# First value block of a hybrid attention block as a seven-product set, with three output gates ahead of it, and a tighter weave of side work

## The chip, the cores and the metric

The kernel runs on one core of a Trainium2 chip. The metric is the device time of one execution in microseconds (us). Matrix products run on TensorE (PE, with PEld for its loads of the stationary operand), element-wise work on VectorE (DVE) and ScalarE (ACT), small work and some DMA issues on GpSimd (POOL), and most DMA issues on SyncE (SP).

## What is computed

One layer over 256 tokens `x` of width 2048, with 256 context tokens `ctx` as a second source. All projections come from one matrix `w_in` with 19,456 columns.

```python
xn = rmsnorm(h, norm_gain[l]) * (1.0 + scale) + shift
cn = rmsnorm(hc, norm_gain[l]) * (1.0 + scale_c) + shift_c
aq, ak, av, ag, hq, hff, hfb, hi, hg, ma, mb = split_columns(xn @ w_in[l])
caq, cak, cav, cag, chq, chff, chfb, chi, chg, cma, cmb = split_columns(cn @ w_in[l])
q = apply_axial_rope(aq...) * q_scale ;  k = apply_axial_rope(ak...)
att_branch = window_attention(q, k, v, k_c, v_c, sink_logits[l]) * jax.nn.silu(ag)
g_f, k_f = hgrn_forget(hff, lb_f_all[l])          # and g_b, k_b; cg_f, ck_f; cg_b, ck_b
v_h, cv_h = to_heads(hi), to_heads(chi)
s_f = hgrn2_final_state(ck_f, cv_h, cg_f)         # start states from the context, both directions
o, _, _ = hgrn2_bidir(q_h, v_h, k_f, g_f, k_b, g_b, s_f, s_b)
hg_branch = hgrn_readout(o, hgrn_norm_gain[l], hg)
h = h + gate * merge_and_project(att_branch, hg_branch, ma, mb, ...)
return rmsnorm(h, final_norm_gain)
```

`hgrn2_bidir` is a gated linear recurrence over 16 heads in both directions, `silu(hg)` its output gate. The values `hi` are needed for the tokens and the context (512 tokens), the output gates, the merge gates `ma`, `mb` and the queries `aq` for the 256 tokens alone.

## The kernel before

**Exact products in three parts.** Every operand is split into a high part (ACT, L85: `wh`) and the rest (DVE, L86: `wl`), and a product is high x high + high x low + low x high. `proj_tok_g` (L108) computes 512 columns for some token tiles of 128: eight chunks, each one load of 512 KB by SP, one `wh`, one `wl`, and six matmuls per token tile and 128-row slice pair (L100, L101 with `wh`, L103 with `wl`). A chunk for two token tiles is a *two-token chunk*, for four a *four-token chunk*. Sums build up in PSUM banks tagged `pj`.

**Seven-product sets.** `quad_tok` (L687) computes 512 columns for all four token tiles with the seven products of Strassen's scheme in place of eight: sums of token halves, `S`, are made once by `token_sums` (DVE L586, L583, on ACT and DVE), sums of the weights by `combos` (L616), split by L635 and L636, multiplied by L732, L734 and L737 in 336 matmuls of 256 columns.

**The stages.** After the set-up of `x` and `ctx` come, in this order on PE (its order is written out by hand from L744): the first forget gates, the first value block `bv0` (512 columns, four token tiles), output gate 0 (two-token chunks; `sgg` at L535), five seven-product sets, then the other forget gates as sets. Then come eight *pairs* (two heads each, `pair`, L797, n = 0 to 7), and at the end the attention and the output projections.

**A pair.** PE transposes decay factors (`tw`), makes the context's end state (`sb`, L952), and then two *level groups* of small matmuls (L872; `al`) that build the causal matrix of the recurrence by doubling: `grow(b)` for b = 1 to 64 multiplies decay totals into `A` (DVE, two L918 for each b from 2 on), `copies` and `keep` (ACT and DVE L887) move the results. `level` 8 to 64 needs `grow` up to 32. `kt` (L978) transposes `A`, so it stands behind `grow(64)`. Then `own` (L993), DVE's L998, and `ob` (L1010 to L1012), the output.

**The weave.** `weave` (L1044) fills the places between these steps with side work for other stages: the `yield` values of `pair` are units of 12,288 PE columns, a two-token chunk is half of one. The side work (`side_work`, L1184) is a list of blocks of eight two-token chunks and one closing entry: output gates 1 to 3, merge gates (`merge_out`), attention queries (`attn_queries`: its result is rotated by DVE L1080, L1085, L1088, written to memory, and fetched back as a *task*, `tkt` at L1104) and attention gates. `SIDE` tells how many entries a pair takes; four chunks of the next pair's query projection (L154, L157) follow. Beside them run: `load_forgets`, whose `ctx_decay` issues the scans L790, L794 and L795 on DVE; `tasks_on`, at fixed entries of a pair (rotated tiles are fetched by POOL, L1139, turned by PE L1104 and written out); and the *gate steps*, one L204 on DVE for each 1.25 units of filler, each with a 256 KB fetch by POOL (`hgw`). In these pairs a query block's rotation stands where its eighth chunk falls.

Of the kernel before, what the change touches and what calls it, by code (L numbers as in the profile page):

```python
# [7 lines left out]
F32 = mybir.dt.float32  # L8
F32R = mybir.dt.float32r
U8 = mybir.dt.uint8  # L10
AF = mybir.ActivationFunctionType
# [3 lines left out]
P = 128  # L15
# [6 lines left out]
PRIO = 100000  # L22

C_Q, C_K, C_V, C_G = 0, 2048, 2560, 3072
C_HQ, C_FF, C_FB, C_HI, C_HG = 5120, 7168, 9216, 11264, 13312
# [13 lines left out]
def block_kernel(ctx: ExitStack, tc: tile.TileContext, x, c, cx, c_ctx, w_ada, b_ada, norm_gain, w_in,  # L39
                 b_merge, lb_f, lb_b, hg_gain, w_oh, sink, w_oa, w_out, fin_gain, cst, msk, out):  # L40
    nc = tc.nc
    pe, act, dve, pool = nc.tensor, nc.scalar, nc.vector, nc.gpsimd
# [6 lines left out]
    fp = ctx.enter_context(pl("fp", side="right"))  # L49
# [77 lines left out]
    def proj_tok(*a):  # L127
        return result(proj_tok_g(*a))
# [389 lines left out]
    def run(g):  # L518
        for _ in g:
            pass  # L520
# [3 lines left out]
    def send():  # L524
        while outs:
            o = outs.pop(0)
            nc.scalar.dma_start(*o[:2])
            tasks.extend(o[2:])

    def output_gate(g):  # L530
        bg = yield from proj_tok_g(w_in, C_HG + 512 * g, x_st, range(2))
        for t in range(2):
            sg = base.tile([P, 512], F32, tag="sm", name="sgg", bufs=3)
            act.activation(sg, bg[t], AF.Sigmoid)
            dve.tensor_tensor(sg, bg[t], sg, op=ALU.mult)  # L535
            outs.append((hg_dr[g][:, t * 512: (t + 1) * 512], sg))
# [24 lines left out]
    with pl("sp", reuse_waits="tile") as sp:  # L561
# [8 lines left out]
        def token_sums(g):  # L570

            def a(h, kh):
                return [X[:, 8 * kh + 4 * g: 8 * kh + 4 * g + 4, :].rearrange("p k (a h t) -> p k a h t", a=2, h=2)
                        [:, :, :, h, :].bitcast(F32) for X in (xH, xL)]

            def v(t):
                return t.rearrange("p (k a t) -> p k a t", k=4, a=2)

            def put(i, t):
                ks = slice(4 * g, 4 * g + 4)  # L580
                dst = [S[:, z, i, ks, :].rearrange("p k t -> p (k t)") for z in range(2)]
                act.activation(dst[0], t, AF.Copy)
                dve.tensor_tensor(dst[1], t, dst[0].bitcast(F32), op=ALU.subtract)  # L583

            def step(out, x_, y_, op):
                dve.tensor_tensor(out, x_, y_, op=op)  # L586

            a11, a12, a21, a22 = a(0, 0), a(0, 1), a(1, 0), a(1, 1)
            p, q = tmp(), tmp()
            step(v(p), a21[0], a22[0], ALU.add)  # L590
            step(v(q), a21[1], a22[1], ALU.add)
            step(p, p, q, ALU.add)
            put(0, p)
            step(v(q), v(p), a11[0], ALU.subtract)
            step(v(q), v(q), a11[1], ALU.subtract)
            put(1, q)
            for i, b in ((3, a12), (2, a22)):
                step(v(p), b[0], v(q), ALU.subtract)
                step(v(p), v(p), b[1], ALU.add)
                put(i, p)  # L600
# [141 lines left out]
                nc.gpsimd.dma_start(dst[t], out[t].rearrange("p a c -> p (a c)"))  # L742

        with tc.manual_schedule(engines={mybir.EngineType.PE}):  # L744
            bv0 = proj_tok(w_in, C_HI, x_st, range(4))
            for g in range(2):
                token_sums(g)
            for t in range(2):
                vo = fp.tile([P, 2, 512], F32, tag="F0", name="vo", bufs=2)
                with tc.high_priority(2 * PRIO):  # L750
                    act.activation(vo[:, 0, :], bv0[t], AF.Copy)
                    dve.tensor_copy(vo[:, 1, :], bv0[2 + t])
                nc.gpsimd.dma_start(v_dr[0][t], vo.rearrange("p a c -> p (a c)"))
            run(output_gate(0))
            send()
            for g in range(1, 4):
                quad_tok(C_HI + 512 * g, v_dr[g])
            for i, co in enumerate((C_K, C_V)):
                quad_tok(co, kv_dr[i])
            for n in range(1, 8):  # L760
                for d in range(2):
                    if (d, n) != (0, 1):
                        quad_col(d, 2 * n)
# [33 lines left out]
    def pair(g, p, F, banks_q):  # L797
# [137 lines left out]
                    pe.transpose(tw[:, (2 * i + s) * P: (2 * i + s + 1) * P], E[d][:, i, s * P: (s + 1) * P], ident)  # L935
            act.activation(wT[:, 4 * d: 4 * d + 4, :], tw.rearrange("p (a b) -> p a b", a=4), AF.Copy)
        copies(1)
        yield 2.0

        for f in done:  # L940
            f()
# [25 lines left out]
        grow(64)  # L967
        for z, b in enumerate((0, 1, 2, 4)):
            keep(a1, z * P, b)
        yield 4.0  # L970
        a3, a4 = al_bank(), al_bank()
        for al, c0, b in ((a3, 0, 8), (a3, P, 16), (a3, 2 * P, 32), (a4, 0, 64)):
            level(al, c0, b)
# [68 lines left out]
    STEP = 24 * 512  # L1042
# [82 lines left out]
    def attn_values():  # L1125
        for t in range(4):
            vr = base.tile([P, 512], F32, tag="sm", name="vr", bufs=3)
            nc.gpsimd.dma_start(vr, kv_dr[1][t % 2][:, (t // 2) * 512: (t // 2 + 1) * 512])
            yield
            rows = slice(8 + 2 * t, 10 + 2 * t)  # L1130
            with behind_chunk():
                split(XH[:, rows, :], XL[:, rows, :], vr.rearrange("p (r c) -> p r c", r=2))
            yield
# [48 lines left out]
        return F  # L1182

    def side_work():  # L1184
        values, NB = attn_values(), 19
        tasks.extend(attn_keys(z, t) for z in range(2) for t in range(2))
        blocks = (output_gate(1), merge_out(0, 0), output_gate(2), attn_queries(0), merge_out(0, 1), output_gate(3),
                  attn_queries(1), merge_out(0, 2), attn_gates(0), merge_out(0, 3), attn_queries(2), merge_out(1, 0),
                  attn_gates(1), merge_out(1, 1), attn_queries(3), merge_out(1, 2), attn_gates(2), merge_out(1, 3),
                  attn_gates(3))  # L1190
        for n, g in enumerate(blocks):
            for k, got in enumerate(g):
                yield got
                if outs and k == 0:
                    with behind_chunk():
                        send()
                if n > NB - 3:
                    next(values, None)
            yield 0
        send()  # L1200

    side = side_work()
    SIDE = (20, 20, 20, 20, 20, 20, 20, 31)

    def inputs(n, res):

        units, F, at = 0, None, [2.5, 5, 6.5, 8]
        steps = load_forgets(n + 1) if n < 7 else iter(())
        for i in range(SIDE[n]):
            if i in (7, 10, 13, 16):  # L1210
                tasks_on()
            got = next(side, None)
            if got is None:
                break
            units += got
            if at and units >= at[0] * STEP:
                at.pop(0)
                next(steps, None)
            yield got
        if n < 7:  # L1220
            F = result(steps)
            res[:] = [F, (yield from proj_col_x_g(w_in, C_HQ + 2 * (n + 1) * HD))]
        else:
            run(side)

    def with_gates(filler):

        for got in filler:
            count[0] += got
            if count[0] >= 1.25 * STEP:  # L1230
                count[0] -= 1.25 * STEP
                with tc.issue_after(last_lo[0]):
                    next(gate, None)
            yield got
# [330 lines left out]
```

## Time and profile before

| what | value |
|---|---|
| median of 3 runs | 1592.65 us (1592.23 to 1593.92) |
| profiled execution | 1593.52 us, span 1591.7 us |
| PE busy | 1567.9 us, 99% of the span |
| PEld busy | 1341.4 us, 84% |
| DVE busy | 1182.9 us, 74% |
| ACT busy | 855.4 us, 54% |
| POOL busy | 140.5 us, 9% |
| HBM traffic | 332 MB, 209 GB/s over the span |

The profile's times are of one execution. A row of the timeline has the start, the busy time, the engine, line and operation, what it writes and reads, and in brackets how long the engine was idle before and what ended that. Instructions on PE and DVE overlap by some tenths of a microsecond, so that the distance of two starts is the price of one in a packed row.

### The profile page before, as it was taken

How to read it: one execution, taken by the hardware profiler on the slowest of the kernel's cores; microseconds unless marked ns; L12 is line 12 of the kernel's file. 1: busy time of each engine (PE TensorE's matmuls, PEld its weight loads, DVE VectorE, ACT ScalarE, POOL GpSimd, SP SyncE). 2: the span in 40 equal slices, each digit the busy share in tenths (PEclk: the TensorE clock that was granted, in tenths of full speed). 3: DMA queues.
4: the chain of work that ended last, by engine and by line, in shares of the span. 5: the costliest groups of instructions: out<-in, count | busy, mean ns of one | idle time of the engine just before them, and what ended most of it. 6: DMA issues, size and time to landing. Idle time of an engine off the chain costs nothing. (4 is left out here: it accounts for less than half of the span.)

```text
span 1591.7 us, 27553 instructions
## 1 busy us (share of the span) xinstructions
PE 1567.9 (99%) x10810; PEld 1341.4 (84%) x10810; DVE 1182.9 (74%) x1745; ACT 855.4 (54%) x1338; POOL 140.5 (9%) x280
## 2 busy tenths in 40 slices
PE   7999999999999999999999999999999999999998
PEld 4567899999888888888888888888887888888887
DVE  4449677777888887787978888887976677757764
ACT  4334443333555555655665566666565776744442
POOL 2000000000000000111121212121112000000000
PEclk9999999999999999999999999999999999999999
DMA  9995533434444444777778777787778854458761
GB/s 369 386 387 174 166 110 131 134 131 133 146 133 136 136 135 130 243 234 230 245 264 271 256 259 244 238 271 240 234 262 262 261 165 149 158 175 288 238 196 70
DMA packets 240851, 333.81 MB, mean 210 GB/s; under 512 B 12080, under 2 KB 157904, under 8 KB 239952
## 3 DMA queue, kind: packets, MB, share of 16 engines
q1 hardware_dynamic: 212048, 249.54, 48.1%
q0 software_dynamic: 19168, 64.08, 11.9%
q10 hardware_dynamic: 9504, 18.42, 3.2%
q8 instruction: 85, 1.39, 0.4%
q14 instruction: 46, 0.38, 0.1%
HBM read 300.53 MB, written 31.47 MB: 209 GB/s over the span
## 5 line engine op out<-in xcount | busy, mean ns | idle before, releaser
L85 ACT ACTIVATE wh<-raw 128x1024 fp32r<-128x1024 f32 x292 | 307.5, 1060 | 257.3 <-PE pj L101 179.1
L86 DVE TENSOR_TENSOR wl<-raw,wh 128x1024 fp32r<-128x1024 f32 x292 | 354.4, 1219 | 122.1 <-ACT wh L85 116.2
L100 PE MATMUL pj<-wh,xHL 128*128 128x512 f32 (+1 forms) x832 | 325.0, 392 | 0.7 <-ACT sg L219 0.7
L101 PE MATMUL pj<-wh,xHL 128*128 128x512 f32 (+1 forms) x832 | 320.3, 386 | 0.0
L103 PE MATMUL pj<-wl,xHL 128*128 128x512 f32 (+1 forms) x832 | 218.5, 386 | 0.0
L100 PEld LDWEIGHTS pj<-wh,xHL 128*128 128x128 f32 x832 | 156.9, 189 | 32.7 <-ACT sg L219 1.9
L101 PEld LDWEIGHTS pj<-wh,xHL 128*128 128x128 f32 x832 | 156.9, 189 | 29.9
L103 PEld LDWEIGHTS pj<-wl,xHL 128*128 128x128 f32 x832 | 154.0, 188 | 31.4
L635 ACT ACTIVATE wh<-T 128x1024 fp32r<-128x1024 f32 x69 | 73.2, 1061 | 149.6 <-DVE T L616 74.0
L635 ACT ACTIVATE wh<-raw 128x1024 fp32r<-128x1024 f32 x92 | 96.9, 1054 | 63.7 <-PE pj L734 23.4
L154 PE MATMUL pj<-xHL,wh 128*128 128x512 f32 x512 | 130.3, 395 | 0.6 <-DVE sgm L1073 0.5
L636 DVE TENSOR_TENSOR wl<-raw,wh 128x1024 fp32r<-128x1024 f32 x92 | 112.0, 1218 | 9.2 <-ACT wh L635 9.1
L154 PEld LDWEIGHTS pj<-xHL,wh 128*128 128x128 f32 x512 | 92.4, 189 | 18.0 <-DVE sgm L1073 0.9
L636 DVE TENSOR_TENSOR wl<-T,wh 128x1024 fp32r<-128x1024 f32 x69 | 84.2, 1220 | 29.7 <-ACT wh L635 29.7
L157 PEld LDWEIGHTS pj<-xHL,wl 128*128 128x128 f32 x512 | 69.9, 190 | 5.8 <-issue 0.7
L157 PE MATMUL pj<-xHL,wl 128*128 128x256 f32 x512 | 71.5, 282 | 0.6 <-issue 0.6
L204 DVE SCALAR_TENSOR_TENSOR acc<-hgw,cg,acc 128x512 f32<-128x512 f32 x60 | 44.8, 747 | 32.7 <-DMA hgw<-in_w_ada_dram 32.7
L918 DVE TENSOR_TENSOR A<-A,X 128x512 f32<-128x512 f32 x96 | 61.7, 684 | 1.6 <-ACT Kmt L848 0.7
L541 POOL DMA_DIRECT2D hgw<-in_w_ada_dram x64 | 34.8, 544 | 273.9 <-DVE acc L204 211.0
L660 PE MATMUL pm<-S,wh 128*128 128x512 f32 x224 | 56.8, 395 | 0.5 <-ACT s L667 0.5
L616 DVE TENSOR_TENSOR T<-raw,T 128x1024 f32<-128x1024 f32 x46 | 56.0, 1218 | 0.0
L616 DVE TENSOR_TENSOR raw<-raw 128x1024 f32<-128x1024 f32 x23 | 28.2, 1225 | 34.9 <-DMA raw<-in_w_in_dram 34.9
(356 smaller groups left out, 3017.9 us busy)
## 6 DMA issues: line engine op xcount, KB each, us to landing
raw<-in_w_in_dram SPq DMA_DIRECT2D x300, 512.0 KB, 4.5
raw<-in_w_ada_dram SPq DMA_DIRECT2D x64, 512.0 KB, 8.0
hgw<-in_w_ada_dram POOLq DMA_DIRECT2D x64, 256.0 KB, 4.4
raw<-in_w_o_hgrn_dram SPq DMA_DIRECT2D x32, 512.0 KB, 3.8
raw<-in_w_o_attn_dram SPq DMA_DIRECT2D x32, 512.0 KB, 4.2
raw<-in_w_out_dram SPq DMA_DIRECT2D x28, 512.0 KB, 3.6
F<-F POOLq DMA_DIRECT2D x16, 512.0 KB, 6.8
F<-F ACTq DMA_DIRECT2D x13, 512.0 KB, 4.4
```

The lines of the kernel that those rows point to most:

```text
L85: last_hi[0] = act.activation(h[:, :n], raw[:, :n], AF.Copy).ins
L86: last_lo[0] = dve.tensor_tensor(lo[:, :n], raw[:, :n], h[:, :n].bitcast(F32), op=ALU.subtract).ins
L100: pe.matmul(o, s[0], m[0], start=first, stop=False)
L101: pe.matmul(o, s[1], m[0], start=False, stop=False)
L103: pe.matmul(o, s[0], m[1], start=False, stop=last)
L154: pe.matmul(o.rearrange("p (a t) -> p a t", a=2), h[:, j, cs_], xHL[:, :, k0 + j, :T], start=k0 + j == 0, stop=False)
L157: pe.matmul(o[:, :T], lo[:, j, cs_], xH[:, k0 + j, :T], start=False, stop=k0 + j == KT - 1)
L616: dve.tensor_tensor(o, x_, y_, op=ALU.subtract)
L635: act.activation(h, src, AF.Copy)
L636: dve.tensor_tensor(lo, src, h.bitcast(F32), op=ALU.subtract)
L660: pe.matmul(m_[z].rearrange("p (z a t) -> p z a t", z=2, a=2), h[:, k, :], mv(k), start=fresh and k == 0, stop=False, skip_group_check=True)
L918: dve.tensor_tensor(av, av, f.unsqueeze(3).to_broadcast([P, 2, n2, b]), op=ALU.mult)
```

## The change

The first value block goes through `quad_tok` like the other three, and three output gates instead of one stand ahead of the four sets, with the sums of the token halves behind the first two of them. So `side_work` loses two output gates. A pair takes 18 entries of side work instead of 20 (two blocks of nine), the last 27 instead of 31; the units between a pair's steps are cut to fit (2.0 to 1.75, 4.0 to 3.5); tasks come at entries 5, 9, 13, 17 instead of 7, 10, 13, 16; a gate step comes for each 1.15 units instead of 1.25. Lines behind the first block move up by six: L918 is L912 in the changed kernel, L1080 is L1074, and so on.

```diff
-            bv0 = proj_tok(w_in, C_HI, x_st, range(4))
-            for g in range(2):
-                token_sums(g)
-            for t in range(2):
-                vo = fp.tile([P, 2, 512], F32, tag="F0", name="vo", bufs=2)
-                with tc.high_priority(2 * PRIO):
-                    act.activation(vo[:, 0, :], bv0[t], AF.Copy)
-                    dve.tensor_copy(vo[:, 1, :], bv0[2 + t])
-                nc.gpsimd.dma_start(v_dr[0][t], vo.rearrange("p a c -> p (a c)"))
-            run(output_gate(0))
-            send()
-            for g in range(1, 4):
+            for g in range(3):
+                run(output_gate(g))
+                send()
+                if g < 2:
+                    token_sums(g)
+            for g in range(4):
                 quad_tok(C_HI + 512 * g, v_dr[g])
...
         copies(1)
-        yield 2.0
+        yield 1.75
...
             keep(a1, z * P, b)
-        yield 4.0
+        yield 3.5
...
-        values, NB = attn_values(), 19
+        values, NB = attn_values(), 17
...
-        blocks = (output_gate(1), merge_out(0, 0), output_gate(2), attn_queries(0), merge_out(0, 1), output_gate(3),
+        blocks = (merge_out(0, 0), attn_queries(0), merge_out(0, 1), output_gate(3),
                   attn_queries(1), merge_out(0, 2), attn_gates(0), merge_out(0, 3), attn_queries(2), merge_out(1, 0),
...
-    SIDE = (20, 20, 20, 20, 20, 20, 20, 31)
+    SIDE = (18, 18, 18, 18, 18, 18, 18, 27)
...
-            if i in (7, 10, 13, 16):
+            if i in (5, 9, 13, 17):
                 tasks_on()
...
-            if count[0] >= 1.25 * STEP:
-                count[0] -= 1.25 * STEP
+            if count[0] >= 1.15 * STEP:
+                count[0] -= 1.15 * STEP
```

On PE a pair reads, before, in two-token chunks: five up to `sb`, four, the first level group, eight, the second level group and `kt`, two, `own`, three (two in some pairs), `ob`; 22 in all with the query projection's four. In the changed kernel: five, `sb`, three, level group, seven, level group and `kt`, three, `own`, two, `ob`; 20 in all.

Two places show what that does to DVE's queue. The first is the first value stage, before, where DVE makes the sums of the token halves (L586, L583) between the `wl` (L86) of the four-token chunks:

```order
L86 TENSOR_TENSOR wl<-raw,wh 128x1024
L586 TENSOR_TENSOR T<-xHL,T 128x1024
L583 TENSOR_TENSOR S<-T,S 128x1024
L586 TENSOR_TENSOR T<-T,xHL 128x1024
L86 TENSOR_TENSOR wl<-raw,wh 128x1024
L583 TENSOR_TENSOR S<-T,S 128x1024
L586 TENSOR_TENSOR T<-xHL,T 128x1024
L586 TENSOR_TENSOR T<-T,xHL 128x1024
L586 TENSOR_TENSOR T<-xHL 128x1024
L86 TENSOR_TENSOR wl<-raw,wh 128x1024
L583 TENSOR_TENSOR S<-T,S 128x1024
```

and the same place in the changed kernel, where the `wl` belong to two-token chunks of the output gates:

```order
L86 TENSOR_TENSOR wl<-raw,wh 128x1024
L586 TENSOR_TENSOR T<-xHL,T 128x1024
L583 TENSOR_TENSOR S<-T,S 128x1024
L86 TENSOR_TENSOR wl<-raw,wh 128x1024 x2
L586 TENSOR_TENSOR T<-T,xHL 128x1024
L86 TENSOR_TENSOR wl<-raw,wh 128x1024 x2
L583 TENSOR_TENSOR S<-T,S 128x1024
L86 TENSOR_TENSOR wl<-raw,wh 128x1024
L586 TENSOR_TENSOR T<-xHL,T 128x1024
```

About two `wl` now stand between two passes of the sums, where it was one to every two or three. The second place is pair n = 2, DVE from the last rows of `grow(2)`'s totals to `grow(8)`. L918 with 128x128x4 is grow(4), with 128x64x8 grow(8), up to 128x8x64 for grow(64). Before:

```order
L86 TENSOR_TENSOR wl<-raw,wh 128x1024
L204 SCALAR_TENSOR_TENSOR acc<-hgw,cg,acc 128x512
L86 TENSOR_TENSOR wl<-raw,wh 128x1024
L918 TENSOR_TENSOR A<-A,X_7899 128x128x4 x2
L887 COPY_PREDICATED X_7899<-mk,al 128x4x32
L1107 SCALAR_TENSOR_TENSOR xHL<-tkt,xHL 128x2x256
L887 COPY_PREDICATED X_7899<-mk,al 128x4x32 x2
L918 TENSOR_TENSOR A<-A,X_7899 128x64x8 x2
```

In the changed kernel the rotation of a query block (L1074, L1079, L1082) stands there:

```order
L86 TENSOR_TENSOR wl<-raw,wh 128x1024
L1074 TENSOR_TENSOR qr<-pj,cs 128x512
L1079 TENSOR_TENSOR rt<-pj,cs 128x8x32 x2
L1074 TENSOR_TENSOR qr<-pj,cs 128x512
L1079 TENSOR_TENSOR rt<-pj,cs 128x8x32 x2
L86 TENSOR_TENSOR wl<-raw,wh 128x1024
L204 SCALAR_TENSOR_TENSOR acc<-hgw,cg,acc 128x512
L1082 TENSOR_TENSOR qr<-qr,rt 128x512
L912 TENSOR_TENSOR A<-A,X_8334 128x128x4 x2
L1082 TENSOR_TENSOR qr<-qr,rt 128x512
L881 COPY_PREDICATED X_8334<-mk,al 128x4x32
```

The rotation has come in ahead of grow(4). Further down the same queue, in the changed kernel, stand the rows up to grow(64) (128x8x64), behind which `kt` waits; the names F_8482 and F_8723 are the forget gates of the next pair:

```order
L86 TENSOR_TENSOR wl<-raw,wh 128x1024
L784 SCALAR_TENSOR_TENSOR e<-F_8482,zero 128x255 x2
L204 SCALAR_TENSOR_TENSOR acc<-hgw,cg,acc 128x512
L86 TENSOR_TENSOR wl<-raw,wh 128x1024
L912 TENSOR_TENSOR A<-A,X_8334 128x32x16 x2
L789 SCALAR_TENSOR_TENSOR F_8482<-F_8482,e 128x2x256
L86 TENSOR_TENSOR wl<-raw,wh 128x1024 x2
L788 SCALAR_TENSOR_TENSOR e<-F_8723,zero 128x255 x2
L204 SCALAR_TENSOR_TENSOR acc<-hgw,cg,acc 128x512
L912 TENSOR_TENSOR A<-A,X_8334 128x16x32 x2
L789 SCALAR_TENSOR_TENSOR F_8723<-F_8723,e 128x2x256
L86 TENSOR_TENSOR wl<-raw,wh 128x1024 x2
```

Behind these rows come one more L204 and the two L912 of grow(64). Between the rotation and them stand eight `wl`, four L204, four scans and two L789; before, the rows from grow(4) to grow(64) held three `wl`, one L204, two scans, one L795 and, between them, two L1107 of a task and the two `sgg` of an output gate. In the pairs n = 4 and 6 the rotation stands at the same place, with seven `wl` and three L204 behind it.

## The prediction

> **What bounds the kernel now.** I read the totals first, then TensorE's waits by releaser, then its timeline. The fence holds both: in a row of waits stand the sum, the number and the longest.
>
> ```profile
> PE 1567.9 (99%) x10810; PEld 1341.4 (84%) x10810; DVE 1182.9 (74%) x1745; ACT 855.4 (54%) x1338; POOL 140.5 (9%) x280
> ...
> PE tkt L1104 <- DMA qr<-qr: 2.5, 1, 2.5
> ...
> PE pj L100 <- ACT sg L219: 0.7, 1, 0.7
> ...
> PE pj L154 <- DVE sgm L1073: 0.5, 1, 0.5
> ...
> PE ob L1012 <- DVE X L998: 0.3, 1, 0.3
> ```
>
> PE is busy for 99% of the span; DVE, the next, for 74%. So PE's program is packed, time goes down by what PE no longer does or waits for, and goes up by whatever makes PE wait. The named waits are few and short. The rows of PE and DVE below give prices from start to start, since records overlap.
>
> ```profile
> 142.83 1.98 PE L103 MATMUL pj<-wl,xHL 128*128 128x512 f32 x8
> ...
> 148.27 1.98 PE L103 MATMUL pj<-wl,xHL 128*128 128x512 f32 x8
> ...
> 179.43 1.07 PE L103 MATMUL pj<-wl,xHL 128*128 128x512 f32 x4
> ...
> 182.15 1.07 PE L103 MATMUL pj<-wl,xHL 128*128 128x512 f32 x4
> ...
> 199.37 0.28 PE L732 MATMUL pj<-wh,xHL 128*128 128x256 f32 x1
> 199.49 0.28 PE L734 MATMUL pj<-wh,xHL 128*128 128x256 f32 x1
> ```
>
> A four-token chunk takes 5.44 us (24 matmuls of 512 columns, 0.227 each), a two-token chunk 2.72, a 256-column matmul of a seven-product set 0.12. Next the windows of the first value block, of output gate 0, and of five sets (columns: window, length, then busy us with counts of PE, PEld, DVE, ACT, POOL, then clock, DMA share, GB/s).
>
> ```profile
> 133.00:177.00 44.00, 43.30 (x191) 35.40 (x190) 39.63 (x38) 20.00 (x23) 1.64 (x3) 1.00 0.40 132
> 177.00:199.00 22.00, 21.99 (x97) 17.77 (x97) 13.27 (x12) 8.32 (x9) 1.06 (x2) 1.00 0.66 215
> 199.00:400.00 201.00, 201.00 (x1675) 200.92 (x1674) 150.83 (x146) 78.78 (x82) 4.78 (x9) 1.00 0.40 129
> ```
>
> Five sets in 201.0 us are 40.2 each, with PE never idle, and DVE has room in all three windows.
>
> **The change, part by part.**
>
> *First value block as a set.* Removed: eight four-token chunks, 8 x 5.44 = 43.5 us. Added: 336 matmuls x 0.12 = 40.3. Both lie on PE's path: **-3.2**. The block's first matmul waited 0.7 for the banks that ACT empties (`L100 <- ACT sg`), as it took four banks; what stands there now, a two-token gate, takes two: **-0.7**.
>
> The Trainium skill, "TensorE: Matmul & The Clock Gate", section "Back-to-back issue gap", puts a matmul at its columns over 2.4 plus 2.5 ns, so an estimate by that page is 215.8 and 109.2 ns, and a saving of 41.4 - 36.7 = 4.7 instead of 3.2. The rows here are 5 to 10% longer than that, and the rows decide.
>
> *Two output gates ahead of the sets.* Sixteen two-token chunks move from the pairs at the same 2.72: 0. Their cover is DVE, which now makes the sums of the tokens beside three gates: 22 `wl` and 25 passes over the tokens of the same size, 47 x 1.13 (the price comes below) = 53.1, and some 6 of small work, against 24 x 2.72 = 65.3 of PE. It fits with 6 us to spare; if it didn't, PE would wait for `wl`, at most about 2.
>
> *Tasks four chunks apart, pairs of two whole blocks.* The one long wait, in the last pair:
>
> ```profile
> 1200.93 0.54 POOL L1139 DMA_DIRECT2D qr<-qr  x1 [2.63 <-DMA ag<-sga]
> ...
> 1206.43 1.09 PE L1104 MATMUL tkt<-cs,qr 128*128 128x128 f32 x4 [2.46 <-DMA qr<-qr]
> 1207.17 0.78 PE L100 MATMUL pj<-wh,xHL 128*128 128x512 f32 x1
> 1207.74 0.63 PE L101 MATMUL pj<-wh,xHL 128*128 128x512 f32 x1
> ...
> 1209.77 0.40 PE L100 MATMUL pj<-wh,xHL 128*128 128x512 f32 x1
> 1210.00 0.39 PE L101 MATMUL pj<-wh,xHL 128*128 128x512 f32 x1
> ```
>
> POOL's fetch of `qr` was held 2.63 us by an outgoing DMA that still read its buffer, and PE waited 2.46 for the tile. Behind it the clock fell: the six matmuls from 1207.17 to 1209.77 took 2.60 instead of 6 x 0.227 = 1.36, 1.2 more. Each task is now fetched and used four chunks (10.9 us) apart, and the last pair uses a tile fetched in the pair before: **-3.7**. The 0.5 for `L154 <- DVE sgm` goes as well, since the four chunks of the query projection now always follow two whole blocks: **-0.5**.
>
> *Two chunks fewer a pair.* PE's own work is only moved. The cover shrinks: from `sb` to `kt` PE has ten two-token chunks instead of twelve, 5.44 less. `kt` transposes A, so it waits for the last `grow`, L918 (grow(64)). DVE's prices there, and the margin in the pair from 940 to 1013 us:
>
> ```profile
> 987.99 0.75 DVE L204 SCALAR_TENSOR_TENSOR acc<-hgw,cg,acc 128x512 f32<-128x512 f32 x1 [0.79 <-DMA hgw<-in_w_ada_dram]
> ...
> 989.86 0.97 DVE L887 COPY_PREDICATED X<-mk,al 128x128 f32<-128x128 uint8 x3
> ...
> 995.87 0.69 DVE L795 SCALAR_TENSOR_TENSOR F<-F,e 128x512 f32<-128x512 f32 x1
> 996.47 1.22 DVE L86 TENSOR_TENSOR wl<-raw,wh 128x1024 fp32r<-128x1024 f32 x1
> 997.60 1.29 DVE L918 TENSOR_TENSOR A<-A,X 128x512 f32<-128x512 f32 x2
> 998.81 1.22 DVE L86 TENSOR_TENSOR wl<-raw,wh 128x1024 fp32r<-128x1024 f32 x1
> 999.94 0.75 DVE L204 SCALAR_TENSOR_TENSOR acc<-hgw,cg,acc 128x512 f32<-128x512 f32 x1
> 1000.61 1.22 DVE L86 TENSOR_TENSOR wl<-raw,wh 128x1024 fp32r<-128x1024 f32 x1
> 1001.74 1.26 DVE L794 TENSOR_TENSOR_SCAN e<-F,zero 128x255 f32<-128x255 f32 x2
> 1002.92 1.26 DVE L918 TENSOR_TENSOR A<-A,X 128x512 f32<-128x512 f32 x2
> ...
> 1007.76 0.68 DVE L1080 TENSOR_TENSOR qr<-pj,cs 128x512 f32<-128x512 f32 x1
> 1008.36 0.74 DVE L1085 TENSOR_TENSOR rt<-pj,cs 128x256 f32<-128x256 f32 x2
> 1009.02 0.68 DVE L1080 TENSOR_TENSOR qr<-pj,cs 128x512 f32<-128x512 f32 x1
> ...
> 1011.42 1.28 DVE L1088 TENSOR_TENSOR qr<-qr,rt 128x512 f32<-128x512 f32 x2
> ```
>
> ```profile
> L918 DVE TENSOR_TENSOR A<-A,X x12: 661/684/693, 977.4 to 1003.5; 128x512 f32<-128x512 f32 x12
> ...
> 1008.12 0.46 PE L872 MATMUL al<-Kmt 128*32 128x32 f32 x32
> ...
> 1009.54 0.66 PE L978 MATMUL kt<-cs,A 128*128 128x128 f32 x4
> ```
>
> From start to start: `wl` 1.13, L918 0.60, gate step 0.67, scan 0.59, L795 0.60, three keeps 0.97. L1080 0.60 and two L1085 0.66, so the rotation (L1080 to L1088) of both tiles of a query block is 2 x 1.26 + 1.2 = 3.7. The last two L918 end by 1004.2, `kt` starts at 1009.54: 5.3 of margin, which the two lost chunks alone would just use up.
>
> But the rotation moves too. In this pair it ran after the grows (1007.76). In the changed order every query block of pairs 2, 4 and 6 ends with the third chunk after `sb`, and its rotation stands on DVE between grow(2) and grow(4), ahead of all grows that `kt` waits for. It can't start before that chunk ends, since it reads the banks. From there DVE has, in pairs 4 and 6: 7 `wl` 7.9, ten L918 6.0, rotation 3.7, 3 gate steps 2.0, four scans and two L795 3.6, keeps 0.9: 24.1. In pair 2 one `wl` and one gate step more: 26.0 (the order's rows are with the change). PE has until `kt`: the first level group, seven chunks, the second: 1.42 (1008.12 to 1009.54) + 7 x 2.72 + 1.42 = 21.9. So `kt` waits 2.2, 2.2 and 4.1: **8.5** from DVE's work alone. DVE also waits for others in that stretch:
>
> ```profile
> DVE acc L204 <- DMA hgw<-in_w_ada_dram: 32.7, 21, 4.4
> ```
>
> A gate step waited 4.4 at the longest, 1.6 in the mean (32.7 / 21), 0.79 in the pair shown. The upper end comes from that pair's row of L918: from 977.4 to 1004.2 is 26.8 us; with the rotation, one `wl` and one gate step more (5.5) it is 32.3, against 1009.54 - 977.4 - 5.44 = 26.7 of PE: 5.6 instead of 2.2, so 3.4 more for each of three pairs, 8.5 + 10.2 = 18.7. A DVE that is late no longer waits for most of what it waited for when early, so I stay near the lower end, with 0.79 a pair: 8.5 + 2.4 = **+10.9**. The lower end, should the added work fall into waits that DVE has in any case, is 0. Queued on DVE behind the rotation: `wl`, so PE may wait at a chunk instead of `kt`; the sum is the same. Queued on POOL: the rotated tile's fetch waits for its own write to land, and stands ahead of the next `hgw` fetch and the memsets of `e`, so a gate step of DVE can be late by it; that is what the 0.79 and the 3.4 stand for. On SP's queue the weight loads only change their order with the blocks; no row shows PE or DVE waiting for them in these stages: 0.
>
> *The clock behind these waits.* The 2.46 wait cost 1.2 more. Three waits of 3.0, 3.0 and 4.9 are all longer: 3 x 1.2 = **+3.6**, and 0 if they come in pieces.
>
> The same page of the Trainium skill, section "HAM oscillation — how this bites in real kernels", asks for no PE gap over about 3.4 us. Here 2.46 already was followed by half the clock, so the trace is stricter. By the page only pair 2's wait would be, and the sum 2.4 lower, 1596.6.
>
> *From `own` to `ob`.* Two chunks (5.4) cover L998 instead of three. The only wait known is 0.3 (`ob <- X`): 0, between -0.3 and some 1.4 a pair. *Gate steps each 1.15 units* instead of 1.25 keep their rate per pair: 22 two-token chunks of half a unit / 1.25 = 8.8 steps before, 20 x 0.5 / 1.15 = 8.7 now: 0 beyond the steps counted.
>
> Sum: -3.2 - 0.7 - 3.7 - 0.5 = -8.1; +10.9 + 3.6 = +14.5; together +6.4. The profiled execution took 1593.52 (span 1591.7 and 1.8 around it), 0.87 above the median 1592.65. 1593.52 + 6.4 = 1599.9, against the median **1599.0**.
>
> **Rivals.**
>
> *The cover holds (faster).* One mechanism: DVE's added work fills its present idle time, 26% of the span, and no `kt` waits. For it: this pair's margin of 5.3; the grows have priority. Against: 24.1 and 26.0 of work against 21.9 of cover. It decides at the end of the last grow, 21.9 us behind the rotation's start. Then only -8.1 is left: 1584.5.
>
> *Half covered (no change).* The waits are 8.5 as counted, DVE's own waits vanish, and the clock drops once or not at all: -8.1 + 8.5 = +0.4, with one drop +1.6: 1593.0 to 1594.2. For it: 2.2 is shorter than the one wait behind which a drop is seen.
>
> *The set is no gain.* DVE is late in the first stage and the 3.2 turn into waits for `wl`: 3.2 more on whichever case holds. Against: the 6 us to spare, and five sets in a row without a wait.
>
> **How the numbers follow.** About 0.2%, 3.2 us, is what a measurement of this kernel can tell from no change. The forecast (waits of 9 to 19 in three pairs with clock drops) gets 0.54, the half-covered case 0.21, the covered one 0.25; the third is an addition inside each. Faster 0.25, same 0.21, slower 0.54. The likeliest case alone reaches from 1595 (8.5 of waits, two drops, is 1595.4) to 1607 (18.7 and three drops: 1592.65 - 8.1 + 18.7 + 3.6 = 1606.9). To hold 8 in 10 the range must take in most of the covered case as well, which with a wait of some 1.5 left in one pair is 1586: 1586 to 1606.
>
> **What the changed profile would show.** PE 10,954 instructions instead of 10,810; L100, L101, L103 768 each instead of 832; L732 and L734 672 instead of 560. The waits `tkt <- DMA qr` and `L100 <- ACT sg` gone. New: `kt` waiting for DVE's A at the grow's line, L912 in the new numbering, about 3 us in pairs 4 and 6 and 5 in pair 2, with slow matmuls behind. I am wrong if those waits are missing or below 1 us, if DVE makes PE wait for `wl` before 200 us, or if another pair's `kt` waits as long.

## The result, and the profile after

The changed kernel takes 1609.53 us (median of four runs, 1607.85 to 1610.38) against 1592.44 for the kernel before: 1.0105 times as long, 95% interval 1.0088 to 1.0123, so 17 us slower. The forecast was 1599.0, slower, with a range up to 1606. The profiled span went from 1591.7 to 1608.6, 16.9 more, and the rows below belong to that execution. First the totals and PE's waits (sum, number, longest):

```profile
PE 1568.5 (98%) x10954; PEld 1348.6 (84%) x10954; DVE 1202.5 (75%) x1764; ACT 860.2 (53%) x1344; POOL 141.9 (9%) x280
...
PE kt L972 <- DVE A L912: 8.4, 6, 3.4
...
PE tkt L1098 <- issue: 5.2, 3, 2.2
PE al L866 <- ACT so L842: 3.4, 3, 1.7
...
PE tkt L1098 <- PE sb L946: 0.5, 1, 0.5
```

PE has the 10,954 instructions that were foreseen. The waits `tkt <- DMA qr` and `L100 <- ACT sg` are gone, and three kinds are new: `kt` for the last L912, 8.4; the 64-wide part of the second level group (`al`, L866) for ACT's copy `so` of what a grow has made, 3.4; and `tkt`, 5.2 and 0.5, of which the first carries no releaser. `kt` and `al` hang on the same chain of grows, so they are one term of 11.8.

The first stage did what it should. PE's timeline, the first row of the block that the change replaces, in the kernel before and after, then the first matmul of the sets and of what follows them:

```profile
132.59 0.50 PE L100 MATMUL pj<-wh,xHL 128*128 128x512 f32 x1
```

```profile
134.57 0.50 PE L100 MATMUL pj<-wh,xHL 128*128 128x512 f32 x1
...
200.03 0.28 PE L732 MATMUL pj<-wh,xHL 128*128 128x256 f32 x1
...
441.94 1.32 PE L660 MATMUL pj<-xHL,wh 128*128 128x512 f32 x5
```

Six sets took 441.94 - 200.03 = 241.9, again 40.3 each, and three gates 200.03 - 134.57 = 65.5 where gate and first block took 199.37 - 132.59 = 66.8. From the block's first row to the first L660 it is 307.4 now and was 268.4 (132.59 to 400.97), 39.0 more for sixteen chunks of 2.72: 4.5 saved, where 3.2 + 0.7 were forecast. That the stage began 2.0 later, ahead of anything that the change touches, is part of the 16.9 and none of the change: in the runs below the same row starts anywhere from 132.2 to 134.1.

Where the loss lies: pair 4, DVE and then PE.

```profile
1005.41 0.75 DVE L204 SCALAR_TENSOR_TENSOR acc<-hgw,cg,acc 128x512 f32<-128x512 f32 x1 [2.25 <-DMA hgw<-in_w_ada_dram]
...
1012.15 0.68 DVE L1074 TENSOR_TENSOR qr<-pj,cs 128x512 f32<-128x512 f32 x1
...
1016.41 1.28 DVE L912 TENSOR_TENSOR A<-A,X 128x512 f32<-128x512 f32 x2
...
1035.23 0.75 DVE L204 SCALAR_TENSOR_TENSOR acc<-hgw,cg,acc 128x512 f32<-128x512 f32 x1 [1.07 <-DMA hgw<-in_w_ada_dram]
1035.90 1.29 DVE L912 TENSOR_TENSOR A<-A,X 128x512 f32<-128x512 f32 x2
...
1033.66 0.65 PE L866 MATMUL al<-so,acc 128*32 128x64 f32 x32 [1.23 <-ACT so L842]
1036.64 0.69 PE L972 MATMUL kt<-cs,A 128*128 128x128 f32 x2 [2.33 <-DVE A L912]
```

DVE started the rotation at 1012.15, had the first L912 behind it at 1016.41 and the last at 1035.90. PE came to the 64-wide level at 1032.4 and to `kt` at 1034.3, waited 1.23 and 2.33. Two of DVE's gate steps had to wait for their fetches, 2.25 behind `sb` and 1.07 right ahead of the last grow. In pair 2 `kt` waited 3.36, and this is what follows:

```profile
897.12 1.29 PE L972 MATMUL kt<-cs,A 128*128 128x128 f32 x4 [3.36 <-DVE A L912]
898.06 0.78 PE L100 MATMUL pj<-wh,xHL 128*128 128x512 f32 x1
...
901.62 1.27 PE L103 MATMUL pj<-wl,xHL 128*128 128x512 f32 x4
902.73 0.60 PE L1098 MATMUL tkt<-cs,qr 128*128 128x128 f32 x4
```

One two-token chunk took 902.73 - 898.06 = 4.67 instead of 2.72, that is 2.0 more. With `kt` itself, from its start to the `tkt` behind the chunk, it is 5.61 here and 5.81 in pair 4 (1036.64 to 1042.45), where a later run at full clock takes 3.26 (pair 4 of "One chunk back", 1022.16 to 1025.42): the slow clock cost 2.35 + 2.55 = 4.9. By windows (clock third from the right) two of the three pairs with a rotation ahead of the grows show it, and pair 6 doesn't:

```profile
844.00:918.00 74.00, 69.65 (x594) 58.59 (x593) 58.21 (x96) 40.88 (x74) 16.38 (x32) 0.95 0.76 250
986.00:1058.00 72.00, 68.44 (x584) 57.62 (x583) 57.93 (x95) 40.63 (x73) 14.75 (x29) 0.95 0.74 242
1127.00:1196.00 69.00, 65.99 (x583) 55.77 (x581) 58.11 (x94) 39.56 (x72) 14.16 (x29) 1.00 0.77 254
```

And the term that the prediction did not have, in pair 5: PE, then DVE.

```profile
1072.92 1.95 PE L946 MATMUL sb<-v,X 128*128 128x128 f32 x16
...
1077.11 0.63 PE L1098 MATMUL tkt<-cs,qr 128*128 128x128 f32 x4 [2.24 <-issue]
...
1074.38 1.23 DVE L86 TENSOR_TENSOR wl<-raw,wh 128x1024 fp32r<-128x1024 f32 x1 [0.38 <-ACT wh L85]
...
1076.53 0.48 DVE L1030 SCALAR_TENSOR_TENSOR bL<-to,cols,bH 128x256 fp32r<-128x256 f32 x1
```

`tkt` stands right behind `sb` now and waited 2.24. It is written into the PSUM bank that `to`, the output turned a chunk earlier, was in; DVE's second L1030, which reads `to`, was queued behind a `wl` and others, and ran at 1076.53 to 1077.01, and `tkt` started at 1077.11. In this trace the row names no releaser; both tiles have the tag `tp` in the kernel, and in a later run the releaser is named.

### The profile page after: what moved, and what is told of

It reads as the page before. It is cut to its first block, busy times and chain, and to the rows that moved or that the text cites. A ratio compares the mean times of both kernels' runs of the same rounds, so it can differ in the third digit from the quotient of the medians.

```text
span 1608.6 us, 27869 instructions
## 1 busy us (share of the span) xinstructions
PE 1568.5 (98%) x10954; PEld 1348.6 (84%) x10954; DVE 1202.5 (75%) x1764; ACT 860.2 (53%) x1344; POOL 141.9 (9%) x280
## 5 line engine op out<-in xcount | busy, mean ns | idle before, releaser
L86 DVE TENSOR_TENSOR wl<-raw,wh 128x1024 fp32r<-128x1024 f32 x284 | 344.1, 1219 | 111.1 <-ACT wh L85 109.9
L100 PE MATMUL pj<-wh,xHL 128*128 128x512 f32 (+1 forms) x768 | 300.4, 393 | 0.0
L101 PE MATMUL pj<-wh,xHL 128*128 128x512 f32 (+1 forms) x768 | 296.7, 388 | 0.0
L103 PE MATMUL pj<-wl,xHL 128*128 128x512 f32 (+1 forms) x768 | 203.3, 386 | 0.0
L100 PEld LDWEIGHTS pj<-wh,xHL 128*128 128x128 f32 x768 | 145.5, 189 | 28.8 <-ACT sg L219 0.6
L101 PEld LDWEIGHTS pj<-wh,xHL 128*128 128x128 f32 x768 | 145.6, 190 | 28.1
L103 PEld LDWEIGHTS pj<-wl,xHL 128*128 128x128 f32 x768 | 142.7, 189 | 29.3
L635 ACT ACTIVATE wh<-T 128x1024 fp32r<-128x1024 f32 x75 | 79.5, 1061 | 164.0 <-DVE T L616 70.5
L154 PE MATMUL pj<-xHL,wh 128*128 128x512 f32 x512 | 130.4, 396 | 0.0
L636 DVE TENSOR_TENSOR wl<-raw,wh 128x1024 fp32r<-128x1024 f32 x100 | 121.7, 1217 | 10.4 <-ACT wh L635 10.4
L636 DVE TENSOR_TENSOR wl<-T,wh 128x1024 fp32r<-128x1024 f32 x75 | 91.5, 1220 | 32.4 <-ACT wh L635 32.4
L154 PEld LDWEIGHTS pj<-xHL,wh 128*128 128x128 f32 x512 | 92.1, 189 | 16.6
L204 DVE SCALAR_TENSOR_TENSOR acc<-hgw,cg,acc 128x512 f32<-128x512 f32 x60 | 44.6, 744 | 25.3 <-DMA hgw<-in_w_ada_dram 25.1
L912 DVE TENSOR_TENSOR A<-A,X 128x512 f32<-128x512 f32 x96 | 61.6, 682 | 0.3
L616 DVE TENSOR_TENSOR T<-raw,T 128x1024 f32<-128x1024 f32 x50 | 60.9, 1218 | 0.1
L660 PE MATMUL pj<-S,wh 128*128 128x512 f32 x208 | 52.6, 395 | 0.8 <-ACT s L667 0.6
```

The source lines that it names most:

```text
L86: last_lo[0] = dve.tensor_tensor(lo[:, :n], raw[:, :n], h[:, :n].bitcast(F32), op=ALU.subtract).ins
L100: pe.matmul(o, s[0], m[0], start=first, stop=False)
L101: pe.matmul(o, s[1], m[0], start=False, stop=False)
L103: pe.matmul(o, s[0], m[1], start=False, stop=last)
L154: pe.matmul(o.rearrange("p (a t) -> p a t", a=2), h[:, j, cs_], xHL[:, :, k0 + j, :T], start=k0 + j == 0, stop=False)
L616: dve.tensor_tensor(o, x_, y_, op=ALU.subtract)
```

## The experiments

Each is timed in five rounds beside the kernel before on its own chip; the medians of before differed from series to series (1593.9 to 1596.5 us), so results are given as ratios to it. 0.1% is 1.6 us.

**The shorter cover alone.** In the kernel before, two chunks go from between the level groups to ahead of `sb`.

```diff
-        yield 2.0
+        yield 3.0
...
-        yield 4.0
+        yield 3.0
```

> Edit: the kernel before, with two chunks moved from between the level groups to ahead of sb (yields 3.0 and 3.0 instead of 2.0 and 4.0): the cover of the changed kernel, with all else as before. Theory (the cover from sb to kt decides): kt waits 3 to 5 us in pairs 0 and 6, whose stretches hold rotations, 1 to 2 in pairs 1 and 2, 10 to 15 above before with the slow clock. Rival (only a whole rotation ahead of the grows makes kt late, as in pairs 2, 4 and 6 of the changed kernel): no more than 5 above before.

1.0141 (1.0126 to 1.0156), 22 us slower than before, with no set, no moved block and no new task entry.

```profile
PE kt L978 <- DVE A L918: 7.4, 5, 3.8
...
PE tkt L1104 <- DVE bL L1036: 4.3, 1, 4.3
PE al L872 <- ACT so L848: 2.5, 2, 2.1
PE pj L100 <- ACT wh L85: 2.4, 1, 2.4
```

`kt` and the level group wait 9.9 in all. In pair 1 `tkt` now follows `to` directly, and the trace names what it waits for: `bL`, L1036, which reads `to`. So the loss comes with the cover alone, and the rival, that it takes the whole rotation ahead of the grows, is out: pair 2 has no rotation in this stretch, and its `kt` waits 1.45. The longest waits, 3.9 in pair 0 and 4.2 in pair 6 with the level group's, are in pairs that do have a rotation among their grows, as the theory said. The loss was more than either side expected, since the wait of `tkt` and one for a `wh` (2.4) came with it.

**One chunk back, ahead of the level groups.** In the changed kernel one chunk goes from ahead of `sb` to behind the first level group.

```diff
-        yield 1.75
+        yield 1.25
...
-        yield 3.5
+        yield 4.0
```

> Edit: the changed kernel with one chunk moved from ahead of sb to between the level groups, nothing else; tkt then stands one chunk behind sb. Theory (in pairs 2, 4 and 6 the rotation ahead of the grows makes kt late; its distance to kt stays as it was, since the chunk is added ahead of it): kt still waits there, 8 to 12 us in all with its slow clock, while the four waits at tkt (6.4) and pair 0's (1.4) go: 8 to 10 above before. Rival (the length from sb to kt decides, not where the rotation stands): kt's waits go as well, 5 to 8 below before.

0.9942 (0.9930 to 0.9953): 9 us *faster* than before, the best of all versions. The rival was right and the theory as stated wrong. Pair 4 of this kernel, DVE and then `kt`:

```profile
999.61 1.29 DVE L912 TENSOR_TENSOR A<-A,X 128x512 f32<-128x512 f32 x2
...
1001.69 0.68 DVE L1074 TENSOR_TENSOR qr<-pj,cs 128x512 f32<-128x512 f32 x1
...
1020.87 1.27 DVE L912 TENSOR_TENSOR A<-A,X 128x512 f32<-128x512 f32 x2
...
1022.16 0.66 PE L972 MATMUL kt<-cs,A 128*128 128x128 f32 x4
```

The rotation still stands in the stretch, but grow(4) (999.61) now comes ahead of it. From its start to the end of the last L912 (1020.87 + 1.27) DVE takes 20.5 instead of 25.0 (1012.15 to 1035.90 + 1.29): part of the work that the count from the rotation charged to the time behind it gets done ahead of it, and a gate step's fetch holds DVE for 0.7 there where it was 1.1. The grows end at 1022.14, `kt` starts at 1022.16, unhindered: all cover is used up. `tkt` stands a chunk behind `sb` here, and does not wait either. PE's waits between 670 and 1260 us that the list names have sunk to 0.3 at the longest.

**Two chunks back.** The same with 0.75 and 4.5.

> Edit: the changed kernel with two chunks instead of one moved from ahead of sb to between the level groups (yields 0.75 and 4.5). With one chunk no kt waited over 0.5 us, the grows ended 0.2 to 1.0 us ahead of kt in pairs 2, 4 and 6, and the time was 9.5 below before. Theory (cover was all that lacked): the margins grow to about 3 us, no time is gained, 8 to 10 below before. Rival (the three chunks left ahead of sb are too few for to and the copies of tw): sb or tkt wait 1 to 2 us a pair, 5 below to 5 above before.

1.0009 (1.0000 to 1.0017): the gain is gone. No `kt` lacks grows any more, but the step ahead does:

```profile
PE to L1024 <- DVE so L1016: 3.6, 3, 2.4
PE to L1024 <- DVE redg L212: 2.3, 1, 2.3
```

Three chunks between `tw` and `sb` are too few for the output that is turned there: `to` waits for the output tile of the pair before, and for the reduction tile of the gate vectors that held its bank. The rival holds, with waits for `to` in place of `sb`. So one chunk more between `sb` and `kt` pays, and a second one, taken from ahead of `sb`, costs more than it brings.

**The tasks alone.** In the changed kernel:

```diff
-            if i in (5, 9, 13, 17):
+            if i in (7, 10, 13, 17):
```

> Edit: the changed kernel with the tasks at entries 7, 10, 13, 17 instead of 5, 9, 13, 17, so that tkt stands two chunks behind sb and not right behind it. Theory (tkt behind sb waits for to to be read out of their shared bank, and that is lost time): the four waits (6.4) go and the time is 10 to 11 above before. Rival (DVE's pace: kt and the level groups wait for as much more): 14 to 17 above before, with kt's waits at 17 us or more instead of 13.

1.0070 (1.0055 to 1.0084) against 1.0105: 5.6 us less (the two intervals together leave about 3.6 either way), as the theory had it.

```profile
PE kt L972 <- DVE A L912: 7.9, 8, 3.2
...
PE al L866 <- ACT so L842: 3.2, 3, 1.9
...
PE tkt L1098 <- DMA kr<-kv: 2.1, 1, 2.1
```

The four waits of `tkt` for `to` are gone, and `kt` and `al` wait 11.1 where it was 11.8. One fetch is late instead (`kr`, 2.1), since two tasks are three entries apart now. So the tasks right behind `sb` cost about 6 us, and the shorter cover with the rotation in it the rest.

**Blocks exchanged.** The query block of pairs 2, 4 and 6 goes behind the merge gate block, and its rotation to the pair's end.

```diff
-                  attn_queries(1), merge_out(0, 2), ...
+                  merge_out(0, 2), attn_queries(1), ...
```

> Edit: in pairs 2, 4 and 6 the query block changes places with the merge gate block behind it, so that its rotation falls to the pair's end; the tasks of pairs 3, 5 and 7 follow one entry later, so that no tile is turned right behind sb there. Theory (the rotation in front of the grows makes kt late; tkt behind sb waits for its PSUM bank): the waits at the second level group and kt of pairs 2, 4 and 6 (4.3 + 4.0 + 3.2 us) and the slow clock behind them (4.9) go, and three of four waits at tkt (1.3 + 2.4 + 2.0): 1609.5 - 16.4 - 5.7 = 1587. Rival (the two lost chunks alone make kt late, wherever the rotation stands): waits of about 2 us stay in each pair, some 1600.

1.0045 (1.0032 to 1.0059), 10 us better than the changed kernel, but 7 above before where 5 below was expected. That is the rival's time (some 1600), but not by its mechanism. The waits at `kt` in pairs 2, 4 and 6 are gone as foreseen, so less DVE work in the stretch does what more cover does; but others have come:

```profile
PE tkt L1098 <- DVE redg L212: 6.1, 1, 6.1
PE kt L972 <- DVE redg L212: 2.9, 1, 2.9
PE kt L972 <- DVE A L912: 2.3, 2, 2.1
```

The reduction of the gate vectors (`redg`, L212) reads a bank that `tkt`, or once `kt`, is written to next, and now falls directly ahead of them.

**Rotation held back.** Blocks as in the changed kernel; DVE's rotation ordered behind the pair's last grow.

```diff
...
+                if late and k == 6:
+                    with tc.issue_after(last_grow[0]):
+                        late.pop()()
...
```

> Edit: blocks in the order of the changed kernel, but in pairs 2, 4 and 6 DVE may start the rotation only behind the last grow of the pair, and its result is sent seven chunks later (so that the tasks of pairs 3, 5 and 7 also come one entry later). Theory: as with the blocks exchanged, 1587. Rival (the rotation holds two of four pj banks for seven chunks more, and the next block or the query projection waits for a bank): waits of some us at the block's first matmul in three pairs, 1595 to 1605.

1.0055 (1.0042 to 1.0069), much the same as with the blocks exchanged and by the same waits, and the rival's wait for a bank that the rotation holds (`L154 <- rt`) is real, but 3.0 in all; the time is in the rival's range:

```profile
PE tkt L1098 <- DVE redg L212: 6.3, 1, 6.3
...
PE pj L154 <- DVE rt L1079: 3.0, 2, 1.6
PE kt L972 <- DVE redg L212: 2.7, 1, 2.7
```

**Chunk from behind `kt`.** One chunk goes from between `kt` and `own` to between the level groups (3.5 to 4.0, 1.25 to 0.75).

> Edit: one two-token chunk moves from between kt and own to between the level groups (3.5 to 4.0, 1.25 to 0.75); the rotation stays where it is. Theory: every wait at kt shrinks by 2.7 us or goes (13.5 to about 3.3) and no clock drop stays (4.9): 1609.5 - 10.2 - 4.9 = 1594; the waits at tkt stay at 6.4. Rival (the chunk is only moved, and own and ob wait in turn for ACT's copy of kt and DVE's state, up to 2.7 in each pair): 1600 to 1610.

1.0061 (1.0047 to 1.0074). `kt` waits as little as the theory said, yet only half of the gain arrives, and the time is in the rival's range:

```profile
PE tkt L1098 <- issue: 10.4, 3, 5.0
...
PE al L987 <- ACT X L878: 3.7, 1, 3.7
PE kt L972 <- DVE A L912: 1.8, 4, 1.1
```

`own` waits once for an ACT copy, as the rival said, and `tkt` behind `sb` twice as long as before: PE reaches it earlier, and DVE doesn't.

**Banks.** `to` in a level bank instead of `tkt`'s:

```diff
-            to = ps.tile([P, 2, 2, HD], F32, tag="tp", name="to")
+            to = ps.tile([P, 2, 2, HD], F32, tag=alt(), name="to")
```

> Edit: the transposed output tile of the pair before (to) takes one of the two level banks instead of the bank that it shares with tkt. Theory (tkt waits until DVE has read to out of the shared bank): the four waits at tkt (0.65 + 1.3 + 2.4 + 2.0 = 6.4 us) go and nothing else changes, 1603. Rival (tkt waits for the fetched tile qr, which lands late): no change, 1609.5. Second rival (the level banks are held instead): the waits turn up at the first level group or at tw, 1609.5 or more.

1.0097 (1.0082 to 1.0113), no measurable gain.

```profile
PE kt L972 <- DVE A L912: 7.2, 7, 3.4
...
PE sc L92 <- DVE mx L1313: 4.0, 1, 4.0
```

`tkt` doesn't wait any more, so the shared bank was its cause, but `kt` waits as before and the attention behind the pairs now waits 4.0, whose banks take turns with the level banks; the edit has shifted these turns, so the gain is not cleanly measured here. With `to` (in all pairs but the last) and `tqg`, the tile that `redg` reads, in `pj` banks (`bank("to")`, `bank("tqg")`):

> Edit: the changed kernel with to and tqg on pj banks, blocks in their order. Theory (shared banks): the four waits at tkt go, 6.4 us less than the changed kernel, so 10 to 11 us above before. Rival (DVE's pace): the waits at tkt go and kt, the level groups and the attention behind the pairs wait for as much more, 15 to 17 us above before.

1.0086 (1.0068 to 1.0105), 14 above before and between the two.

```profile
PE kt L972 <- DVE A L912: 9.0, 8, 4.1
...
PE al L866 <- ACT so L842: 5.2, 3, 2.0
PE pj L154 <- DVE hsum L165: 5.0, 3, 2.7
```

The waits for `to` have become waits of the query projection's first matmul for a `pj` bank (5.0). The same with the blocks exchanged:

> Edit: the exchanged blocks, and besides the turned output tile (to) and the gate vectors' reduction tile (tqg) take one of the four pj banks instead of the banks that tkt and kt use. With the blocks exchanged alone the time was 7 us above before; the waits left there were kt behind the reduction (3.1), tkt behind the reduction (6.2), tkt behind to (0.65) and the slow clock after them (4.7). Theory (shared banks pass DVE's delays on to PE): these 14.7 go, 7 us below before (ratio 0.995); the wait at kt of pair 0 stays. Rival (DVE's pace: what PE doesn't wait for there it waits for a little later): at least half comes back, within 1 us of before or slower.

1.0051 (1.0034 to 1.0069), no better than the exchange alone:

```profile
PE pj L154 <- DVE hsum L165: 10.5, 3, 4.3
```

The attention gates' blocks use all four `pj` banks, and `to` takes one of them. The Trainium skill, "Perfetto Trace Analysis", section "Matmuls", advises that independent matmul groups rotate through different PSUM banks so that emptying one overlaps the next group. Here every bank has an owner, so a tile that leaves one queue joins another, and these three runs show no gain clear of noise; the next one, which moves the reduction tile alone, does.

**The reduction tile alone on `pj`, with blocks exchanged**, `to` where it was:

> Edit: exchanged blocks and tqg on a pj bank, without the moved chunk. With the blocks exchanged alone 7 us above before, with waits of 3.1 (kt) and 6.2 (tkt) for the reduction and 4.7 of slow clock after them. Theory (shared bank): those 14 go, 5 to 7 below before; pair 0's wait at kt (2.3) and its slow clock stay. Rival (DVE is late there in any case, and PE waits for wl or kt instead): 0 to 5 above before.

0.9982 (0.9968 to 0.9995): 10 us better than the exchange alone where 12 to 14 were expected, and 3 below before. With the one chunk ahead of `sb` moved as well:

> Edit: exchanged blocks, the chunk moved from ahead of sb to between the level groups (yields 1.25 and 4.0), and only the reduction tile of the gate vectors (tqg) on a pj bank; to stays in the bank of tkt. The kernel that had to on pj as well was 1 us below before, with 3.8 and 3.5 us of waits at the query projection for that bank and 1.6 of slow clock. Theory (with DVE's rotation out of the stretch and eleven chunks of cover no kt waits, and without a shared bank between to, tqg and the side work's blocks nothing else does): 8 to 10 us below before, ratio 0.994. Rival (tqg on pj collides with the attention gates' blocks, which take all four banks): waits of 2 to 4 us in pairs 5 and 7, no better than 3 below before.

0.9968 (0.9956 to 0.9980), 5 below before where 8 to 10 were expected. The one long wait left in the pairs, with 3.41 us at half clock behind it, is at the end of the gate steps:

```profile
PE tgr L555 <- DVE gcol L214: 3.3, 1, 3.3
```

and the same with `to` on a `pj` bank too:

> Edit: exchanged blocks and pj banks as above, and one two-token chunk moves from ahead of sb to between the level groups (yields 1.25 and 4.0 instead of 1.75 and 3.5). Theory: from sb to kt PE has eleven chunks of cover, so no kt waits longer than 0.5 us in any pair; 2 to 4 us below the same kernel without this edit, some 10 below before. Rival (the chunk lost ahead of sb makes sb or the tiles behind it wait instead): no gain over the kernel without it.

0.9990 (0.9977 to 1.0004): 10 us better than without the moved chunk, but 2 below before where some 10 were expected: no `kt` waits, and two waits for `to`'s bank stay:

```profile
PE pj L154 <- DVE bL L1031: 6.8, 2, 3.6
```

**DVE's load.** The changed kernel with 15 of 16 gate steps and their fetches left out:

```diff
+                if k0 == 0:
                     gate_chunk(accT[:, 0, :], g, k0)
```

> Edit: the changed kernel with 15 of 16 gate steps left out, each with its fetch (so the output's gate vector lacks them); about nine steps of 0.67 us a pair, and DVE's waits for their fetches, are gone from DVE's queue in every pair; the order of blocks, banks and tasks stays. Theory (PE's waits in the pairs come from DVE's load): of the 20 us of waits and 5 of slow clock in the pairs less than 5 are left, 3 us below before or lower. Rival (the waits hang on where the rotation and the tasks stand, and DVE's load counts only by the 2 to 3 us of steps in a stretch): kt still waits in pair 2, the four waits at tkt stay, 3 to 8 us above before.

0.9951 (0.9934 to 0.9968), 8 us below before, 25 below the changed kernel, with its order untouched. All that is left:

```profile
PE tkt L1099 <- issue: 3.5, 3, 1.2
```

So it is DVE's lateness that PE waits for in the pairs. Whether the steps' own time makes DVE late or its waits for their fetches, this run doesn't tell, since it leaves out both: in the changed kernel these fetches held DVE for 2.0, 3.3 and 0.9 us between `sb` and the last grow of pairs 2, 4 and 6. That `tkt` still waits some 1.2 three times, within the theory's 5, is the bank again: in pair 3 DVE's second L1031 ends at 926.83, and `tkt` starts at 926.93.

## Why the prediction was wrong

**Right.** The direction, and the mechanism it named: two chunks of cover less and a rotation ahead of the grows make `kt` late. The count was good to a microsecond: from the rotation's start to the end of the last grow DVE took 26.7, 25.0 and 23.9 us in pairs 2, 4 and 6, where 26.8, 24.9 and 24.9 were reckoned with the fetches, and the waits at `kt` and the level group there were 3.9, 3.6 and 2.8 for 4.9, 3.0 and 3.0. The gains are there: 40.3 for a set, the waits for `qr` and `sg` gone. The chunk moved back brings 9 us, against the 8.1 that the covered case was priced at.

**The step that failed: the tasks.** "Each task is now fetched and used four chunks apart" looked at the fetch alone. The same table entry, 5 instead of 7, puts the use, `tkt`, directly behind `sb`, one chunk behind `to`, whose bank it shares; that was nowhere in the sum. It cost 5.7 by the waits and 5.6 by the run that moves the tasks alone. With it in the sum the forecast would have been 1604.7; the run that moves the tasks alone is by its ratio at 1603.6, inside the range.

**Terms of the wrong size.** The waits of the grows were put at 10.9 and were 11.8, of which 1.17 lies in pair 0, put at nothing: there DVE had stood 2.21 for an outgoing `sgm`. That is as long as `kt` itself waits in pair 6, so the sign "another pair's `kt` waits as long" did show. The slow clock was put at 1.2 behind each of three waits; it was 2.35 in pair 2, 2.55 in pair 4 and none in pair 6: 4.9 instead of 3.6. Of the 16.9, then, -8.1, 11.8, 5.7, 4.9 and the 2.0 of the late beginning make 16.3; the last 0.6 are not placed.

**The rule on the clock.** By the 3.4 us of the Trainium skill ("TensorE: Matmul & The Clock Gate", section "HAM oscillation — how this bites in real kernels") only waits longer than that would be followed by the slow clock. Pair 2's 3.36 was, as was the 1.23 with 2.33 of pair 4, while 2.24 at `tkt` in pair 5 was not. So the length of one wait alone doesn't tell. The traces show what does: in each of them all changes of the granted clock lie whole multiples of 3.41 us apart (pair 2's stretch at half clock runs from 895.20 to 902.03, pair 4's from 1035.14 to 1041.97, 41 steps later). With time cut into these steps, what counts is PE's idle time within one:

| step | PE idle | clock in the next step |
|---|---|---|
| before, 1202.79 to 1206.20 | 2.23 | 0.50 |
| after, pair 2, 891.78 to 895.20 | 1.94 | 0.50 |
| after, pair 4, 1031.73 to 1035.14 | 2.06 | 0.50 |
| after, pair 5, 1072.69 to 1076.10 | 1.23 | 1.00 |
| after, pair 5, 1076.10 to 1079.51 | 1.01 | 1.00 |
| after, pair 7, 1212.64 to 1216.05 | 1.82 | 1.00 |

Between 450 and 1330 us of all sixteen traces the clock fell 31 times, each time behind a step with 1.89 us or more of idle time, and no step at full clock that it didn't follow had more than 1.90. Pair 5's 2.24 fell on two steps, and so did pair 6's 1.67 and 1.17 (1.5 in each).

**A reason that was too narrow.** The prediction counted DVE's work from the rotation's start, with the distance from there to `kt` as the cover. The chunk moved ahead of the level groups lies outside that distance, as the changed order puts it ahead of the rotation's start, and removes the wait all the same. What counts is all of DVE's work between `sb` and the last grow against all of PE's: ten chunks were too few for this work, eleven are just enough.

**What stays open.** The waits are not additive: what one edit takes from `kt` comes back at `tkt` (10.4 with the chunk from behind `kt`). How the 17 us divide between cover and rotation can't be told to the microsecond; a chunk more of cover, or the rotation out of the stretch, is each enough to remove the waits at `kt` in pairs 2, 4 and 6.

## What to carry to other kernels

When filler is taken out of a packed engine's order, count for each stretch the work of the slower engine that must end in it against the cover left, from one dependency to the next, and try how one chunk more or less in each place does: here one chunk in eight pairs is the difference between 1% slower and 0.6% faster. An entry in a table that moves a task moves its use as well as its fetch, and a use has a bank with a reader on another engine's queue. Moving a tile to another bank helps only where that bank has nobody waiting.

## What was not expected of the hardware

The clock fell behind waits of 2.3 to 3.4 us at `kt` and not behind one of 2.24 at `tkt`: it went by the idle time within a step of 3.41 us, some 1.9 in these traces, so that a wait of the same length can cost nothing more or, with one or two steps at half clock behind it, another 1.2 to 2.6 us.
